# Stick-breaking attention in a hybrid block: three score banks, one out-projection bank, pairs finished by ScalarE and GpSimd

## The chip, the cores and the metric

The kernel runs on one core of a Trainium2 chip. The metric is the time of one execution on the device in microseconds, as the median of several runs. The core's engines are PE (TensorE, whose weight loads are shown as PEld), DVE (VectorE), ACT (ScalarE), POOL (GpSimd) and SP (SyncE, which here issues all DMAs of the kernel in one queue).

## What is computed

One decoder layer over 2048 tokens of width 1024, all in float32: an RMS norm, one input projection whose columns feed three mixers (a convolution branch, a gated unit with position mixing, and an attention of 8 heads of 64), an RMS norm of each branch, one output projection with a residual, then a gated feed-forward part and a final norm. The change acts in the attention and in the output projection behind it. Attention is of the stick-breaking kind:

```
z = q @ k.T * scale                      # scores of a 128-query block against all earlier keys
log_1m_beta = where(mask, -softplus(z), 0)
log_a = -softplus(-z) + reverse_cumsum(log_1m_beta) - log_1m_beta
a = where(mask, exp(log_a), 0)           # mask: strictly causal
o = a @ v
y = concat([rms(y_a), rms(y_b), rms(o)]) * g_out
x = x + y @ w_out
```

## The kernel before

Every matmul operand is split into a high and a low part, and each product is three matmuls (`mm3`, lines 114 to 117) or, with k and v, two. The work goes through stages, with tile pools opened and closed between them.

The first stage treats the sequence in two halves of 1024 tokens. For each it projects the columns of the two other mixers, then k, q and v, and stores q, k and v (as differences of neighbouring rows) to DRAM tensors `qh_d`, `ql_d`, `kh_d`, `kl_d` and `v_d`. When the second half is done, the operands of the first attention pair are loaded into four tiles `pre` of the pool that held x (lines 513 to 550), the outstanding pieces of the other branches are emitted, and the pools change.

The attention stage (lines 553 to 904) has 80 units: four blocks `qs` of 512 queries, four pairs `pr` of heads, chunks `kc` of 512 keys from the last to the first, and the two heads of the pair. Each unit has four steps, so there are 320 in one written order (loop at line 855). A step does three things. `front` (L709) makes a 128x512 block of scores in a PSUM bank of pool `zp` by two matmuls (L726, L729); ScalarE takes 1 - sigmoid of it into `om` (L731), and VectorE scans it along the keys (L739, or L734 with the mask on the diagonal chunk). The scan reads the bank, so it frees it. Six steps later `transpose_a` (L746) transposes a 128-key column of the four blocks of a unit and splits it into `ah` and `al`, the low part by VectorE from PSUM for even columns (L764) and by GpSimd from a copy for odd ones (L761). Eight steps later (`LAG_V`) `times_v` (L767) adds the products with v to one of two banks `po`, one for each head of the pair.

When a pair is through all its key chunks, `finish_pair` (L776) adds the two halves of each head's bank (ScalarE copies one, L783, VectorE adds the other, L784), adds `vend` (GpSimd, L787), scales by g_out and splits into `ych` and `ycl` (ScalarE L794, VectorE L795), stores both, and adds the squares to `sq` (ScalarE L802, VectorE L803). After four pairs `rms_c` turns `sq` into the branch's norm.

Between the steps the output projection runs as a filler: `out_proj` (L640) is a generator that emits three matmuls at a time into a bank `pab` of pool `opp`; after four such pieces VectorE adds the bank into the tile `x1` (L667 for the first two branches, L669 for attention). A debt of 0.6 pieces a step (1.8 in steps 14 to 31) decides when a piece is emitted, and a piece is issued behind the latest scores. What is left after the last step is emitted in one go (line 898), and the last block of attention's output projection follows (lines 901 and 975). A second generator, `down_blocks` (L592), runs every 20 steps from step 40 on: it loads two row blocks of w_down into tiles `wd0` and `wd1`, forms four combinations on GpSimd and stores them.

The program is written in this order, but each engine's queue is ordered by a list scheduler that simulates the time line, so that an instruction that is ready can be put ahead of ones written before it. Semaphores are placed by the framework. PSUM has eight banks: in this stage two each for scores (`zp`), output projection (`opp`), transposes (`atp`) and products with v (`otp`).

Of the kernel before, what the change touches and what calls it, by code (L numbers as in the profile page):

```python
# [15 lines left out]
P = 128  # L16
# [4 lines left out]
def kernel(  # L21
# [412 lines left out]

    for hf in range(2):
# [31 lines left out]
        for c0, hd, ld in ((1536, kh_d, kl_d), (1024, qh_d, ql_d)):  # L467
            w = load_w(c0)
            for ct in range(NPAIR):
# [43 lines left out]
    def load_q(tiles, qs, pr):  # L513
        qA, qB = tiles
        t_s = slice(qs * 512, (qs + 1) * 512)
        dma32(qA[0:64], qh_d[pr, 0:64, t_s])
        dma32(qA[64:128], ql_d[pr, 0:64, t_s])
        dma32(qB[0:64], ql_d[pr, 64:128, t_s])
        dma32(qB[64:128], qh_d[pr, 64:128, t_s])
        return tiles  # L520

    def load_kv(tiles, kc, pr):
        kA, kB, lA, lB, vv = tiles
        k_s = slice(kc * 512, (kc + 1) * 512)
        for hd, th_, tl_ in ((0, kA, lA), (1, kB, lB)):
            hr = slice(64 * hd, 64 * hd + 64)
            for r in (slice(0, 64), slice(64, 128)):
                dma32(th_[r], kh_d[pr, hr, k_s])
                dma32(tl_[r], kl_d[pr, hr, k_s])
        dma32(  # L530
            vv,
            v_d[kc * 4 : kc * 4 + 4, :, pr * 256 : (pr + 1) * 256].rearrange(
                "n p c -> p n c"
            ),
        )
        return tiles


    pre = [
        xp.tile([P, D], F32R, tag="xi", name=f"pre{i}").rearrange("p (a c) -> p a c", a=2)  # L540
        for i in range(4)
    ]
    first_q = load_q((pre[0][:, 0, :], pre[0][:, 1, :]), 0, 0)
    first_kv = load_kv(
        (
            pre[1][:, 0, :], pre[1][:, 1, :], pre[2][:, 0, :], pre[2][:, 1, :],
            pre[3].rearrange("p a (n c) -> p (a n) c", c=256),
        ),
        0, 0,
    )  # L550
# [8 lines left out]
    tp2 = pool(cr, "tp2", 3, "right")  # L559
    co = ExitStack()  # L560
    opp = pool(co, "opp", 2, "right", space=PSUM)
    zp = pool(cr, "zp", 2, "right", space=PSUM)
# [20 lines left out]
    def load_wo(f):  # L583
        raw = xo.tile([P, D], F32, tag="xo", name="rawo", bufs=3)
        nc.sync.dma_start(raw, w_out_r[f])
        wh = wo.tile([P, D], F32R, tag=f"woh{f}", name=f"woh{f}")
        wl = wo.tile([P, D], F32R, tag=f"wol{f}", name=f"wol{f}")
        split_pool(wh, wl, raw)
        wo_h.append(wh)
        wo_l.append(wl)  # L590

    def down_blocks():  # L592

        for f in range(NFH):
            r0 = xo.tile([P, D], F32, tag="wd0", name="wd0", bufs=1)
            r1 = xo.tile([P, D], F32, tag="wd1", name="wd1", bufs=1)
# [38 lines left out]
    def load_x1(n, g):  # L635
        x1 = xo.tile([P, D], F32, tag="xo", name="x1", bufs=3)
# [3 lines left out]
    def out_proj(qs, g, kept=()):  # L640
# [6 lines left out]
        for j in range(4):  # L647
            n = qs * 4 + j
            x1, (yh, yl) = nxt, ys.pop(0)
            for nh in range(2):  # L650
# [5 lines left out]
                ps = opp.tile([P, 512], F32, tag="opp", name="pab")  # L656
# [18 lines left out]
                if nh == 1 and g == 1:  # L675
# [99 lines left out]

    def finish_pair(p, sq):  # L776
        pr = p.pr
        yp = tp2.tile([P, 512], F32, tag="tmp", name="yp", bufs=2)
        tmp = tp2.tile([P, 512], F32, tag="tmp", name="tmp", bufs=2)
        for hd in range(2):  # L780
            hr = slice(64 * hd, 64 * hd + 64)
# [12 lines left out]
        A.mul(ych, yp, gc)  # L794
        V.scalar_tensor_tensor(ycl, yp, gc, ych, op0=ALU.mult, op1=ALU.subtract)  # L795
# [481 lines left out]
```

## Time and profile before

| | |
|---|---|
| median of 3 runs | 2570.83 us (2569.0 to 2572.99) |
| profiled execution, its own time | 2562.59 us |
| its span | 2560.5 us |
| TensorE clock granted, mean | 0.978 |
| PE busy | 2412.8 us (94%) |
| PEld busy | 1962.2 us (77%) |
| DVE busy | 1853.6 us (72%) |
| ACT busy | 1203.6 us (47%) |
| POOL busy | 1226.9 us (48%) |
| DMA moved | 445.68 MB |

The profile is one execution, its times are counted from the start of the span. Busy time of PE is modelled, since matmuls overlap in the array: a matmul of 512 columns is shown with about 0.39 us, but the next begins after 0.23 us. The share of a whole span says little here, as the stages have different limits; the attention stage lies between about 518 and 1190 us.

### The profile page before, as it was taken

To read this page: it belongs to the slowest core of one execution; us is meant where nothing else is said; L and a number is where in the kernel's file an instruction comes from. 1 tells how busy PE (TensorE), PEld (TensorE's weight loads), DVE (VectorE), ACT (ScalarE), POOL (GpSimd) and SP (SyncE) were. 2 spreads that over 40 slices of the span, in tenths; PEclk is the share of its full clock that TensorE was granted. 3 is DMA by queue.
4 is the path that set the end of the run, shared out by engine and by line. 5 is a ranking of instruction groups with operands and counts; after the bars stand their busy time and mean duration, and the time that the engine had idled before them with its cause. 6 is when DMAs were issued, how large, how long until landed. Compare 5 with 4: busy or idle time off the path is not lost.

```text
span 2560.5 us, 33221 instructions
## 1 busy us (share of the span) xinstructions
PE 2412.8 (94%) x11139; PEld 1962.2 (77%) x11139; DVE 1853.6 (72%) x2344; ACT 1203.6 (47%) x2130; POOL 1226.9 (48%) x929
## 2 busy tenths in 40 slices
PE   7999999968889899998799999999989999999998
PEld 5878778756767777777588888888877888888887
DVE  3881595357789899994588988875557888888555
ACT  4333522365567677773444444454344344345542
POOL 2434552454447647653144444565433444447551
PEclk9999999978999999999899999999999999999999
DMA  4245625399999898866433333397643333337962
GB/s 138 83 147 173 190 83 156 131 257 267 272 269 269 268 264 243 243 203 205 145 95 107 108 95 105 116 334 231 173 162 106 100 107 103 99 107 224 304 191 91
DMA packets 418073, 445.68 MB, mean 174 GB/s; under 512 B 24018, under 2 KB 301790, under 8 KB 417903
## 3 DMA queue, kind: packets, MB, share of 16 engines
q1 hardware_dynamic: 417903, 443.55, 58.6%
q8 instruction: 89, 1.46, 0.2%
q14 instruction: 81, 0.66, 0.1%
HBM read 305.57 MB, written 137.89 MB: 173 GB/s over the span
## 4 chain that ended last, share of the span: by engine, by line
PE 76%; DMA 9%; DVE 6%; POOL 3%; ACT 3%; issue 3%; SPq 1%; POOLq 0%; ACTq 0%; DVEq 0%
PE prod L116 11%; PE prod L115 11%; PE prod L117 11%; PE pd L116 6%; PE pd L115 6%; PE pd L117 5%; PE pjt L115 3%; PE pjt L117 3%; PE pjt L116 3%; PE pat L752 3%; DVE om L739 2%; PE pz L726 2%; PE po L774 1%; PE pjd L115 1%; PE pjd L116 1%
## 5 line engine op out<-in xcount | busy, mean ns | idle before, releaser
L121 POOL TENSOR_TENSOR wl<-raw,wh 128x512 fp32r<-128x512 f32 (+1 forms) x260 | 381.8, 1470 | 566.6 <-ACT wh L120 542.0
L115 PE MATMUL prod<-thh,wh 128*128 128x512 f32 x1232 | 482.9, 392 | 6.4 <-DVE thl L1008 5.8
L116 PE MATMUL prod<-thl,wh 128*128 128x512 f32 x1232 | 485.8, 394 | 0.3 <-DVE thl L1008 0.3
L117 PE MATMUL prod<-thh,wl 128*128 128x512 f32 x1232 | 482.5, 392 | 0.0
L120 ACT CAST wh<-raw 128x512 fp32r<-128x512 f32 (+1 forms) x260 | 178.0, 686 | 318.2 <-PE prod L116 178.2
L121 POOL TENSOR_TENSOR dwl<-raw,dwh 128x512 fp32r<-128x512 f32 x154 | 221.6, 1469 | 135.6 <-ACT dwh L120 95.6
L115 PEld LDWEIGHTS prod<-thh,wh 128*128 128x128 f32 x1232 | 232.1, 188 | 61.3 <-DVE thl L1008 7.8
L761 POOL TENSOR_TENSOR al<-ar,ah 128x512 fp32r<-128x512 f32 (+2 forms) x160 | 188.2, 1178 | 177.1 <-ACT ah L760 126.7
L116 PEld LDWEIGHTS prod<-thl,wh 128*128 128x128 f32 x1232 | 232.2, 188 | 50.6 <-DVE thl L1008 1.1
L117 PEld LDWEIGHTS prod<-thh,wl 128*128 128x128 f32 x1232 | 232.2, 188 | 48.9
L739 DVE TENSOR_TENSOR_SCAN om<-om,pz 128x512 f32<-128x512 f32 x192 | 239.6, 1270 | 36.4 <-ACT om L731 35.2
L116 PE MATMUL pd<-dwl,sah 128*128 128x512 f32 x616 | 242.1, 393 | 0.0
L115 PE MATMUL pd<-dwh,sah 128*128 128x512 f32 x616 | 240.8, 391 | 1.1 <-DVE thl L1008 1.0
L117 PE MATMUL pd<-dwh,sal 128*128 128x512 f32 x616 | 240.6, 391 | 0.0
L1126 DVE TENSOR_TENSOR sal<-ar,sah 128x512 fp32r<-128x512 f32 x168 | 154.2, 930 | 119.1 <-ACT sah L1125 108.5
L1066 DVE SCALAR_TENSOR_TENSOR cv<-u,vec,cv 128x1024 f32<-128x1024 f32 x176 | 222.6, 1287 | 14.1 <-ACT cv L1064 12.3
L731 ACT ACTIVATE om<-pz 128x512 f32<-128x512 f32 (+2 forms) x320 | 168.2, 545 | 89.9 <-PE pz L729 88.0
L1013 DVE TENSOR_TENSOR u<-prod,u 128x512 f32<-128x512 f32 x220 | 147.2, 686 | 64.2 <-PE prod L117 61.0
L752 PE MATMUL pat<-ident,om 128*128 128x128 f32 x1088 | 180.1, 281 | 8.7 <-DVE al L764 3.9
L752 PEld LDWEIGHTS pat<-ident,om 128*128 128x128 f32 x1088 | 138.5, 144 | 43.9 <-DVE al L764 7.6
L121 POOL TENSOR_TENSOR wl<-s,wh 128x512 fp32r<-128x512 f32 x88 | 122.7, 1394 | 98.0 <-ACT wh L120 98.0
L734 DVE TENSOR_TENSOR_SCAN om<-om,mask 128x128 f32<-128x128 f32 (+3 forms) x128 | 142.2, 1140 | 34.9 <-ACT om L731 34.6
(278 smaller groups left out, 5167.5 us busy)
## 6 DMA issues: line engine op xcount, KB each, us to landing
raw<-in_w_up_dram SPq DMA_DIRECT2D x88, 512.0 KB
ar<-s_d SPq DMA_DIRECT2D x112, 256.0 KB
s_d<-act SPq DMA_DIRECT2D x110, 256.0 KB
raw<-in_w_in_dram SPq DMA_DIRECT2D x40, 512.0 KB
raw<-wd_d SPq DMA_DIRECT2D x40, 512.0 KB
vv<-v_d SPq DMA_DIRECT2D x39, 512.0 KB
x_d<-x SPq DMA_DIRECT2D x32, 512.0 KB
raw<-in_w_down_dram SPq DMA_DIRECT2D x30, 512.0 KB
```

The costliest lines, as they stand in the source:

```text
L115: T.matmul(ps, lh, rh, start=start, stop=False)
L116: T.matmul(ps, lh, rl, start=False, stop=False)
L117: T.matmul(ps, ll, rh, start=False, stop=stop)
L120: A.copy(hi, src)
L121: G.tensor_tensor(lo, src, hi, op=ALU.subtract)
L731: A.activation(om, pz[:, :w_], AF.Sigmoid, scale=-0.125)
L739: V.tensor_tensor_scan(om[:, ::-1], om[:, ::-1], pz[:, ::-1], initial=p.carry[hd, j], op0=ALU.mult, op1=ALU.bypass,)
L752: T.transpose(pt[:, j * P : (j + 1) * P], a4[j][:, b * P : (b + 1) * P], ident)
L761: G.tensor_tensor(al[:, c_], ar[:, c_], ah[:, c_], op=ALU.subtract)
L1013: V.tensor_tensor(dst, ps, other, op=ALU.add)
L1066: V.scalar_tensor_tensor(cv, u[:, j : j + HALF], cw(j), cv, op0=ALU.mult, op1=ALU.add)
L1126: V.tensor_tensor(lo, ar, hi, op=ALU.subtract)
```

## The change

Seven edits are made together.

- Pool `zp` gets three banks and `opp` one; `zp` now closes together with `opp`, after the last output projection, whose accumulations (the last query block of attention) use `zp`.
- Finishing is split. `finish_head` runs behind a head's last product with v: ScalarE copies both halves of the bank to SBUF (`tmp` and `yp`), so a bank is read by ScalarE alone. `finish_pair` then adds them on GpSimd, adds `vend`, sums the squares on GpSimd, scales on GpSimd, copies to `ych` on ScalarE and takes the low part on GpSimd. The last pair of all keeps VectorE for these (`is_last`).
- `LAG_V` is 9 in place of 8, and the parts `ah` and `al` have four buffers in place of three.
- The operands of the first pair are loaded before the q projections of the second half rather than after its v projections. The helpers `load_q` and `load_kv` move up with them, unchanged.
- The tiles `wd0` and `wd1` are taken from the tag `xo`, which x1, the raw rows of w_out and `er` share; it has four buffers in place of three, and the two single buffers are gone.
- GpSimd's multiplication of h by `gffn_b` is done in two halves of 512 columns.
- In `finish_pair` the squares come before the scaling.

```diff
--- before.py
+++ after.py
@@ -432,6 +432,31 @@
             )
         dma32(v_d[n], vt.rearrange("p a b d -> p (a b d)"))
 
+    def load_q(tiles, qs, pr):
+        qA, qB = tiles
+        t_s = slice(qs * 512, (qs + 1) * 512)
...
+    def load_kv(tiles, kc, pr):
+        kA, kB, lA, lB, vv = tiles
...
     for hf in range(2):
 
         for ch in range(2):
@@ -466,6 +491,23 @@
 
         for c0, hd, ld in ((1536, kh_d, kl_d), (1024, qh_d, ql_d)):
             w = load_w(c0)
+            if hf == 1 and c0 == 1024:
+
+                pre = [
+                    xp.tile([P, D], F32R, tag="xi", name=f"pre{i}").rearrange(
+                        "p (a c) -> p a c", a=2
+                    )
+                    for i in range(4)
+                ]
+                first_q = load_q((pre[0][:, 0, :], pre[0][:, 1, :]), 0, 0)
+                first_kv = load_kv(
+                    (
+                        pre[1][:, 0, :], pre[1][:, 1, :], pre[2][:, 0, :],
+                        pre[2][:, 1, :],
+                        pre[3].rearrange("p a (n c) -> p (a n) c", c=256),
+                    ),
+                    0, 0,
+                )
             for ct in range(NPAIR):
                 for ch in range(2):
                     ps = proj_t(w, ct, hT[ch])
@@ -510,44 +552,6 @@
             w = load_w(0)
             nxt.append(transpose_x(xs))
             hT = nxt
-    def load_q(tiles, qs, pr):
...
-    def load_kv(tiles, kc, pr):
...
-    pre = [
...
-    first_q = load_q((pre[0][:, 0, :], pre[0][:, 1, :]), 0, 0)
...
     while later:
         tick()
     cr.close()
@@ -556,10 +560,10 @@
     cr = ExitStack()
     kv = pool(cr, "kv", 2, "right")
     ap_ = pool(cr, "ap", 1, "right")
-    tp2 = pool(cr, "tp2", 3, "right")
+    tp2 = pool(cr, "tp2", 4, "right")
     co = ExitStack()
-    opp = pool(co, "opp", 2, "right", space=PSUM)
-    zp = pool(cr, "zp", 2, "right", space=PSUM)
+    opp = pool(co, "opp", 1, "right", space=PSUM)
+    zp = pool(co, "zp", 3, "right", space=PSUM)
     cl.close()
     cl = ExitStack()
     wo = pool(cl, "wo", 1)
@@ -581,7 +585,7 @@
     wo_h, wo_l = [], []
 
     def load_wo(f):
-        raw = xo.tile([P, D], F32, tag="xo", name="rawo", bufs=3)
+        raw = xo.tile([P, D], F32, tag="xo", name="rawo", bufs=4)
         nc.sync.dma_start(raw, w_out_r[f])
         wh = wo.tile([P, D], F32R, tag=f"woh{f}", name=f"woh{f}")
         wl = wo.tile([P, D], F32R, tag=f"wol{f}", name=f"wol{f}")
@@ -592,8 +596,8 @@
     def down_blocks():
 
         for f in range(NFH):
-            r0 = xo.tile([P, D], F32, tag="wd0", name="wd0", bufs=1)
-            r1 = xo.tile([P, D], F32, tag="wd1", name="wd1", bufs=1)
+            r0 = xo.tile([P, D], F32, tag="xo", name="wd0", bufs=4)
+            r1 = xo.tile([P, D], F32, tag="xo", name="wd1", bufs=4)
             nc.sync.dma_start(r0, w_down_r[f])
             nc.sync.dma_start(r1, w_down_r[NFH + f])
             b11, b12, b21, b22 = r0[:, 0:512], r0[:, 512:D], r1[:, 0:512], r1[:, 512:D]
@@ -633,7 +637,7 @@
         return t
 
     def load_x1(n, g):
-        x1 = xo.tile([P, D], F32, tag="xo", name="x1", bufs=3)
+        x1 = xo.tile([P, D], F32, tag="xo", name="x1", bufs=4)
         nc.sync.dma_start(x1, x1_d[n] if g else xt[n])
         return x1
 
@@ -653,7 +657,10 @@
                     ys.append(load_y(n + 2, g, kept))
                 if nh == 1 and j < 3:
                     nxt = load_x1(n + 1, g)
-                ps = opp.tile([P, 512], F32, tag="opp", name="pab")
+                if g == 1 and qs == NQ - 1:
+                    ps = zp.tile([P, 512], F32, tag="zp", name="pab")
+                else:
+                    ps = opp.tile([P, 512], F32, tag="opp", name="pab")
                 for f in range(4):
                     if f < 4 - len(kept):
                         lh, ll = yh[:, f, :], yl[:, f, :]
@@ -685,7 +692,8 @@
                         )
                     else:
                         G.tensor_scalar(h, x1, r, 1.0, op0=ALU.mult, op1=ALU.mult)
-                        G.tensor_tensor(h, h, gffn_b, op=ALU.mult)
+                        for c in (slice(0, 512), slice(512, D)):
+                            G.tensor_tensor(h[:, c], h[:, c], gffn_b[:, c], op=ALU.mult)
                     if j % 2 == 0:
                         even = h
                     else:
@@ -773,38 +781,58 @@
         T.matmul(po[:, c_], vb, ah[:, c_], start=first, stop=False)
         T.matmul(po[:, c_], vb, al[:, c_], start=False, stop=kc == 0 and b == 3)
 
+    def finish_head(p, hd):
+
+        if hd == 0:
+            p.y = [
+                tp2.tile([P, 512], F32, tag="tmp", name=n, bufs=2) for n in ("yp", "tmp")
+            ]
+        yp, tmp = p.y
+        hr = slice(64 * hd, 64 * hd + 64)
+        other = slice(64 * (1 - hd), 64 * (1 - hd) + 64)
+        A.copy(tmp[hr], p.po[hd][other])
+        if is_last(p):
+            V.tensor_tensor(yp[hr], p.po[hd][hr], tmp[hr], op=ALU.add)
+        else:
+            A.copy(yp[hr], p.po[hd][hr])
+
+    def is_last(p):
+        return p.qs == NQ - 1 and p.pr == NPAIR - 1
+
     def finish_pair(p, sq):
         pr = p.pr
-        yp = tp2.tile([P, 512], F32, tag="tmp", name="yp", bufs=2)
-        tmp = tp2.tile([P, 512], F32, tag="tmp", name="tmp", bufs=2)
-        for hd in range(2):
-            hr = slice(64 * hd, 64 * hd + 64)
-            other = slice(64 * (1 - hd), 64 * (1 - hd) + 64)
-            A.copy(tmp[hr], p.po[hd][other])
-            V.tensor_tensor(yp[hr], p.po[hd][hr], tmp[hr], op=ALU.add)
+        yp, tmp = p.y
+        eng = V if is_last(p) else G
         y4 = yp.rearrange("p (j t) -> p j t", j=4)
         ve = vend[:, pr, 4 * p.qs : 4 * p.qs + 4]
-        G.tensor_tensor(y4, y4, ve.unsqueeze(2).to_broadcast([P, 4, P]), op=ALU.add)
+        if not is_last(p):
+            G.tensor_tensor(yp, yp, tmp, op=ALU.add)
+        eng.tensor_tensor(y4, y4, ve.unsqueeze(2).to_broadcast([P, 4, P]), op=ALU.add)
         if p.qs == 0:
 
             G.memset(yp[:, 0:1], 0.0)
         ych = yc.tile([P, 512], F32R, tag="ych", name="ych")
         ycl = yc.tile([P, 512], F32R, tag="ycl", name="ycl")
         gc = gout_c[:, 4 + pr : 5 + pr]
-        A.mul(ych, yp, gc)
-        V.scalar_tensor_tensor(ycl, yp, gc, ych, op0=ALU.mult, op1=ALU.subtract)
-        t_s = slice(p.qs * 512, (p.qs + 1) * 512)
-        dma32(yh_d[4 + pr, :, t_s], ych)
-        dma32(yl_d[4 + pr, :, t_s], ycl)
         if pr == 0:
             A.square(sq, yp)
         else:
             A.square(tmp, yp)
-            V.tensor_tensor(sq, sq, tmp, op=ALU.add)
+            eng.tensor_tensor(sq, sq, tmp, op=ALU.add)
+        if is_last(p):
+            A.mul(ych, yp, gc)
+            V.scalar_tensor_tensor(ycl, yp, gc, ych, op0=ALU.mult, op1=ALU.subtract)
+        else:
+            G.tensor_scalar(yp, yp, gc, 1.0, op0=ALU.mult, op1=ALU.mult)
+            A.copy(ych, yp)
+            G.tensor_tensor(ycl, yp, ych, op=ALU.subtract)
+        t_s = slice(p.qs * 512, (p.qs + 1) * 512)
+        dma32(yh_d[4 + pr, :, t_s], ych)
+        dma32(yl_d[4 + pr, :, t_s], ycl)
         return ych, ycl
 
     def load_vend():
-        er = xo.tile([P, D], F32, tag="xo", name="er", bufs=3)[:NKB, 0 : NPAIR * P]
+        er = xo.tile([P, D], F32, tag="xo", name="er", bufs=4)[:NKB, 0 : NPAIR * P]
         nc.sync.dma_start(
             er, vr_d[1 : S + 1].rearrange("(n p) c -> n p c", p=P)[:, P - 1, :]
         )
@@ -841,7 +869,7 @@
     anchor = [None]
     sqs, rcs = {}, {}
     debt = 0.0
-    LAG_T, LAG_V = 6, 8
+    LAG_T, LAG_V = 6, 9
 
 
     WO_0, WO_S = 2, 3
@@ -889,6 +917,8 @@
             qs, pr, kc, hd = units[u]
             p = pairs[qs, pr]
             times_v(p, kc, hd, b, *parts_t.pop((u, b)))
+            if kc == 0 and b == 3:
+                finish_head(p, hd)
             if kc == 0 and hd == 1 and b == 3:
                 if pr == 0:
                     sqs[qs] = yb_.tile([P, 512], F32, tag="sq", name="sq", bufs=1)
```

## Rows read from the trace of the kernel before

**Rows 1.** Three stretches: us, each engine busy (instructions), granted clock, DMA share, GB/s.
```profile
525.00:775.00 250.00, 210.90 (x1028) 167.63 (x1029) 183.69 (x222) 148.26 (x323) 120.70 (x104) 0.90 1.01 267
775.00:1125.00 350.00, 325.92 (x1744) 261.55 (x1743) 315.88 (x344) 252.25 (x511) 231.68 (x180) 0.99 0.89 253
...
1160.00:1180.00 20.00, 20.00 (x101) 16.63 (x100) 7.05 (x10) 5.58 (x10) 4.24 (x4) 1.00 0.42 146
```
**Rows 2.** The sigmoid alone (L731) in two of them: ACT busy (instructions), then as above.
```profile
525.00:775.00 250.00, 53.81 (x110) 0.90 1.01 267
775.00:1125.00 350.00, 101.72 (x187) 0.99 0.89 253
```
**Rows 3.** Chain of waits, shares by line, from 525 to 775 and from 775 to 1125.
```profile
by line: DMA yh<-yh_d 7.3%; DMA wd<-in_w_down_dram 7.2%; DMA yl_d<-ycl 5.9%; DVE om L734 5.7%; DMA kB<-kh_d 5.4%; SPq L91 4.9%; PE pat L752 4.7%; DMA x<-in_x_dram 3.9%; issue 3.7%; DMA kA<-kh_d 3.4%; DMA yl<-yl_d 3.3%; DMA rawo<-in_w_out_dr
by line: PE pat L752 12.2%; DVE om L739 9.8%; PE pz L726 7.7%; PE po L774 7.0%; PE pz L729 6.5%; PE po L773 6.5%; issue 5.3%; DVE om L734 5.2%; PE pab L115 4.4%; PE pab L117 4.4%; PE pab L116 4.4%; DVE al L764 2.4%; POOL al L761 2.0%; DMA h
```
**Rows 4.** PE's waits from 775 to 1150: us in total, times, longest.
```profile
PE pz L726 <- DVE om L739: 11.8, 21, 3.5
PE po L774 <- POOL al L761: 7.1, 6, 2.6
PE pat L752 <- DVE al L764: 3.4, 4, 1.2
```
**Rows 5.** Groups of VectorE: operation, count, busy us, mean ns, idle before.
```profile
L784 DVE TENSOR_TENSOR yp<-po,tmp 64x512 f32<-64x512 f32 x32 | 21.8, 680 | 5.2 <-ACT tmp L783 4.6
...
L795 DVE SCALAR_TENSOR_TENSOR ycl<-yp,vec,ych 128x512 fp32r<-128x512 f32 x16 | 13.8, 864 | 4.6 <-ACT ych L794 4.6
...
L803 DVE TENSOR_TENSOR sq<-sq,tmp 128x512 f32<-128x512 f32 x12 | 10.6, 886 | 0.0
```
**Rows 6.** Groups of GpSimd, the same columns.
```profile
L423 POOL TENSOR_TENSOR vp<-vp,vs 128x512 f32<-128x512 f32 x16 | 21.2, 1326 | 39.5 <-DMA vp<-vr_d 29.5 <-ACT om L731 7.6 <-ACT xc L367 1.2
L787 POOL TENSOR_TENSOR yp<-yp,vend 128x512 f32<-128x512 f32 x16 | 17.0, 1062 | 30.4 <-DVE yp L784 17.3 <-ACT ah L760 7.1 <-PE pz L729 6.1
...
L687 POOL TENSOR_SCALAR h<-x,r_ffn 128x1024 f32<-128x1024 f32 x12 | 14.1, 1179 | 0.9
```
**Rows 7.** PE's waits from 525 to 775, first and last of eight for engines.
```profile
PE po L774 <- DVE al L764: 6.0, 7, 2.6
...
PE pat L752 <- DVE om L734: 1.4, 3, 0.6
```
**Rows 8.** A wait of ScalarE from 525 to 1190.
```profile
ACT ych L794 <- POOL yp L787: 10.3, 11, 1.9
```
**Rows 9.** Time line of the flush: start, us, instruction; first and last eviction.
```profile
1161.40 0.39 PE L115 MATMUL pab<-woh,yh 128*128 128x512 f32 x1
1161.60 0.69 DVE L667 TENSOR_TENSOR x<-pab,x 128x512 f32<-128x512 f32 x1 [0.67 <-PE pab L117]
...
1173.45 0.69 DVE L667 TENSOR_TENSOR x<-pab,x 128x512 f32<-128x512 f32 x1 [2.54 <-PE pab L117]
```
**Rows 10.** Time line of PE in the last out-projection; the idle time before stands in brackets.
```profile
1197.50 0.50 PE L115 MATMUL pab<-woh,yh 128*128 128x512 f32 x1 [1.52 <-DVE x L669]
```
**Rows 11.** First operands: a load's row (count, ns, first and last start) and the first score.
```profile
L91 SPq DMA_DIRECT2D pre<-qh_d x2: 545/585/625, 296.4 to 299.1; - x2
...
518.52 0.29 PEld L726 LDWEIGHTS pz<-pre,pre 128*128 128x128 f32 x1 [7.63 <-ACT vs L497]
```
**Rows 12.** Issues of w_down's and x1's tiles (as Rows 11), and VectorE's wait for x1.
```profile
L597 SPq DMA_DIRECT2D wd<-in_w_down_dram x11: 333/577/1192, 602.8 to 999.8; - x11
...
L674 SPq DMA_DIRECT2D x_d<-x x32: 319/452/924, 591.2 to 1217.7; - x32
...
DVE x L667 <- DMA x<-in_x_dram: 7.3, 2, 5.0
```
**Rows 13.** Scans with the mask: ns least, median, most of all; and the narrowest group.
```profile
L734 DVE TENSOR_TENSOR_SCAN om<-om,mask x128: 402/1193/2242, 519.6 to 1111.8; 128x128 f32<-128x128 f32 x32, 128x256 f32<-128x256 f32 x32, 128x384 f32<-128x384 f32 x32, 128x512 f32<-128x512 f32 x32
...
L734 DVE TENSOR_TENSOR_SCAN om<-om,mask 128x128 f32<-128x128 f32 x32 | 25.6, 798 | 14.8 <-ACT om L731 14.7
```

More of the change, by code (lines that the diff above doesn't have):

```diff
@@ L433, in v_steps @@
         dma32(v_d[n], vt.rearrange("p a b d -> p (a b d)"))
+    def load_q(tiles, qs, pr):
+        qA, qB = tiles
+        t_s = slice(qs * 512, (qs + 1) * 512)
+        dma32(qA[0:64], qh_d[pr, 0:64, t_s])
+        dma32(qA[64:128], ql_d[pr, 0:64, t_s])
+        dma32(qB[0:64], ql_d[pr, 64:128, t_s])
+        dma32(qB[64:128], qh_d[pr, 64:128, t_s])
+        return tiles
+    def load_kv(tiles, kc, pr):
+        kA, kB, lA, lB, vv = tiles
+        k_s = slice(kc * 512, (kc + 1) * 512)
+        for hd, th_, tl_ in ((0, kA, lA), (1, kB, lB)):
+            hr = slice(64 * hd, 64 * hd + 64)
+            for r in (slice(0, 64), slice(64, 128)):
+                dma32(th_[r], kh_d[pr, hr, k_s])
+                dma32(tl_[r], kl_d[pr, hr, k_s])
+        dma32(
+            vv,
+            v_d[kc * 4 : kc * 4 + 4, :, pr * 256 : (pr + 1) * 256].rearrange(
+                "n p c -> p n c"
+            ),
+        )
+        return tiles
     for hf in range(2):
@@ L468 @@
             w = load_w(c0)
+            if hf == 1 and c0 == 1024:
[11 more added lines that the diff above has]
+                        pre[3].rearrange("p a (n c) -> p (a n) c", c=256),
+                    ),
+                    0, 0,
+                )
             for ct in range(NPAIR):
@@ L512 @@
             hT = nxt
-    def load_q(tiles, qs, pr):
[L514 to L520, printed above, removed]
-    def load_kv(tiles, kc, pr):
-        kA, kB, lA, lB, vv = tiles
-        k_s = slice(kc * 512, (kc + 1) * 512)
-        for hd, th_, tl_ in ((0, kA, lA), (1, kB, lB)):
-            hr = slice(64 * hd, 64 * hd + 64)
[L527 to L536, printed above, removed]
-    pre = [
-        xp.tile([P, D], F32R, tag="xi", name=f"pre{i}").rearrange("p (a c) -> p a c", a=2)
-        for i in range(4)
-    ]
-    first_q = load_q((pre[0][:, 0, :], pre[0][:, 1, :]), 0, 0)
[L544 to L550, printed above, removed]
     while later:
@@ L774, in times_v @@
         T.matmul(po[:, c_], vb, al[:, c_], start=False, stop=kc == 0 and b == 3)
+    def finish_head(p, hd):
[4 more added lines that the diff above has]
+        yp, tmp = p.y
+        hr = slice(64 * hd, 64 * hd + 64)
+        other = slice(64 * (1 - hd), 64 * (1 - hd) + 64)
[6 more added lines that the diff above has]
+        return p.qs == NQ - 1 and p.pr == NPAIR - 1
     def finish_pair(p, sq):
         pr = p.pr
[L778 to L784 removed]
+        yp, tmp = p.y
+        eng = V if is_last(p) else G
         y4 = yp.rearrange("p (j t) -> p j t", j=4)
         ve = vend[:, pr, 4 * p.qs : 4 * p.qs + 4]
[L787 removed]
+        if not is_last(p):
+            G.tensor_tensor(yp, yp, tmp, op=ALU.add)
+        eng.tensor_tensor(y4, y4, ve.unsqueeze(2).to_broadcast([P, 4, P]), op=ALU.add)
         if p.qs == 0:
```

## The prediction

> **What bounds the kernel now.** I read the slices first: the attention stage runs from about 518 to 1190 us, and it is the only place where every edit acts. Then I cut that stage into stretches [rows 1]. From 525 to 775 the DMA engines show a share of 1.01 at 267 GB/s while PE is busy for 210.9 of 250 us; from 775 to 1125 DMA falls to 0.89, and PE (325.9 of 350 us) and VectorE (315.9) are both near full; from 1160 to 1180 PE is busy without a gap and VectorE nearly idle. So there are three different limits. The sigmoid at L731 runs once per step (one 128-query block of scores), so its count gives the pace [rows 2]: 110 in 250 us, 2.27 us a step, then 187 in 350 us, 1.87 us a step. The chain of waits says the same [rows 3]: in the first stretch its largest items are transfers, in the second they are transposes, scans and matmuls in turn, none over 12.2%. In the second stretch PE and VectorE are therefore coupled, and the waits of PE show through what [rows 4]: 11.8 us in 21 times for a scan (L739) to free a score bank, 7.1 us for GpSimd's low parts (L761), 3.4 us for VectorE's (L764).
>
> **The change part by part.** The sum is made against the profiled execution (2562.59 us, span 2560.5, 2.1 us around it); the median of the three runs is 2570.83, 8.2 above it, and I subtract the saving from that.
>
> *Finishing moved off VectorE, and the third score bank.* Per pair VectorE loses two additions of 0.680, one low part of 0.864 and, in three pairs of four, one sum of squares of 0.886 [rows 5]: 1.36 + 0.86 + 0.66 = 2.89 us. Fifteen of 16 pairs change, 43 us in all; the last keeps VectorE. Some seven of them end between 775 and 1150 (L784 stands there 14 times, two a pair), so 20 us there. VectorE's 315.9 us over 187 steps are 1.69 us a step and become about 1.58; PE's 325.9 are 1.74 and stay. VectorE then has slack, PE is the slower one, and a third bank lets it run one block further ahead of the scans. The 11.8 us can go at most; since the longest single wait was 3.5 us, more than a step, I leave 3 and take -9 (bounds 0 and -12). What is late next is PE itself, whose idle time in that stretch is 350 - 326 = 24 us: no more than that can come back there.
>
> *Products with v a step later, four buffers for the parts.* The low parts get 1.87 us more. The row of 7.1 us has six waits, 1.2 on average and 2.6 at most, so the extra step would cover nearly all; with the 3.4 of VectorE's low parts 10.5 us are in reach. But GpSimd gets a burst per pair: a new addition near 1.33 (L423 has its form), the addition of vend as now (1.06), a sum of squares and a low part near 1.33 each, and a multiplication near 0.59 (half of L687's 1.18) [rows 6], 5.6 us in place of 1.06. Fifteen times 4.6 is 69 us on an engine busy for 352 of 600 us [rows 1]. I take a good half, -6 (bounds 0 and -11).
>
> *The same two in the first stretch.* PE waits there for engines in eight rows, 6.0 us down to 1.4, 22.8 in all [rows 7]. With DMA at 1.01 most of what one wait gives back the next transfer takes, as nothing in the change moves fewer bytes. I take -4 (bounds 0 and -20).
>
> *ScalarE.* Per pair two copies of 64x512 more, 0.58 each; the scaled copy becomes a plain one. They lie in ScalarE's idle time (252 of 350 us busy). But ScalarE now waits for GpSimd twice in a pair (square after vend, copy after the multiplication) where it waited once, 10.3 us in 11 times [rows 8], and the sigmoids stand behind it. Score banks that are a block ahead hide most; +2 (bounds 0 and +10, one more such row). That GpSimd's multiplication by gffn_b is cut in halves only lets a low part in between: 0.
>
> *One out-projection bank.* A bank now has to be evicted before the next group of 12 matmuls can begin. I compared the rows of all 53 evictions with the start of the next group: between 775 and 1160 both overlap in four places, 1.1 us together, since the next group comes a step or two later. It bites where the backlog is flushed: PE begins the next group at 1161.40, the eviction of the one before runs from 1161.60 for 0.69 [rows 9], and four of the five evictions there are like that, near 0.9 us each. 4 x 0.9 + 1.1 = +5 with the way of a semaphore (bounds 0, if other matmuls fill the gaps, and +8, if groups come faster). It is on the path, since PE is full there.
>
> *The last out-projection on three banks, the last pair.* The wait of 1.52 us at 1197.5 for an eviction [rows 10] goes and vend is added by VectorE; -2 (bounds 0 and -3).
>
> *First operands ahead of v.* They are not late now: the loads are issued from 296 us on, though they stand behind v in the text, and the first score starts at 518.5 after a wait of 7.63 for the last copy of v (L497), which frees a score bank's space [rows 11]. The edit moves 13 issues past SP's queue at a place where it has room, and that copy stays: 0 (bounds -8, should another bank come first, and +2).
>
> *The tiles of w_down in the pool of x1.* Four buffers for both, before three and two. One block's pair of tiles is held long: 11 loads from 602.8 to 999.8, 40 us apart [rows 12], so two buffers are almost always w_down's and x1 is left with two. A tile of x1 is stored every 20 us (32 from 591.2 to 1217.7) and the next is loaded half a tile ahead, so two should just do: 0; the other end is the second rival below.
>
> Sum: -9 - 6 - 4 + 2 + 5 - 2 = -14 us, 2548.6 for the profiled execution, **2557** for the median.
>
> VectorE's scans that read om and mask from SBUF take 0.402 at the shortest, and those of 128x128 0.798 on average [rows 13]; something holds them for as long again. By the Trainium skill (SBUF — State Buffer, Who interferes with whom) a VectorE instruction with two SBUF inputs contends with a GpSimd instruction that reads SBUF, and the second to start blocks until the first is done. The trace agrees with it, and the rule speaks against the change: with 0.4 us lost in each of 128 scans at the present 352 us of GpSimd work (an estimate from that row), 69 us more would cost VectorE 128 x 0.4 x 69/352 = 10 us, which leaves 33 of its 43; by the rule alone the sum would be some 3 us smaller.
>
> **The rivals.** *The transfers decide.* If SP's queue and the DMA engines set the pace after 775 too (0.89 is not far from 1), VectorE's relief turns into idle time and only the flush and the tail remain, +5 - 2: 2574, within 0.2%. For it speaks the first stretch; against it, that transfers are hardly in the second chain [rows 3]. Chance 0.19.
>
> *GpSimd becomes the wait (slower).* Place: L761's low part queued behind a pair's burst. Price: 4.6 us more burst less the 1.87 of the added step, 2.7 us a pair, and 15 times 2.7 is 41 us on PE, against which the 20 us of the two first terms stay at best half: 41 - 10 = +31 with the +3 of the bank and the tail, near 2602 if every burst stands whole; half of them gives 2585. It decides where GpSimd runs three or more of the five without a low part in between. For it: 232 of 350 us busy already. Against it: the burst waits for ScalarE twice, which lets low parts in. Chance 0.12, at 2585.
>
> *x1 late for its eviction (slower).* With two buffers an x1 load waits for a store of the block before it, the one bank stays full, and PE stands. VectorE waited 7.3 us in two times for x already, 5.0 the longer [rows 12]. Eight tiles late by 3.6 us, less the 14: +15, 2586. Chance 0.09.
>
> *More comes back.* If PE's 24 us of idle time after 775 all go and the first stretch gives 10: -24 - 10 + 5 = -29, 2542. Chance 0.15. My forecast has 0.45.
>
> **How the numbers follow.** Another 0.2%, 5 us, is about what a measurement of this kernel can tell. The forecast's own range is 2548 to 2566; with bounds and rivals 2530 to 2588. Faster: 0.45 and 0.15, 0.60; same: 0.19; slower: 0.21.
>
> **What would show it.** Right: PE's wait for L739 in the second stretch near 3 us and the step under 1.82; VectorE's busy time in the stage about 40 us lower and GpSimd's about 70 higher; gaps near 0.9 between groups in the flush. Wrong: a row of PE waiting for L761 over 15 us, VectorE waiting for x1, a DMA share of 1 throughout, or a first score well before or after 518.5. A step of 1.87 or more after 775 would refute the first two terms.

## The result: slower, and the profile after

The changed kernel takes 2582.92 us (2579.45 to 2586.41, five runs) against 2569.0 us (2561.53 to 2572.99, five runs) of the kernel before beside it: ratio 1.0064, 95% interval 1.0042 to 1.0086. The forecast was 14 us faster; by the medians it came out 14 us slower. The time lies in the outer range (2530 to 2588) and not in the forecast's own (2548 to 2566), and it moved the other way. The profiled execution took 2586.41 us, its span is 2584.7, 24.2 longer than the one of before, at a mean granted clock of 0.975. The two profiled executions thus stand further apart than the medians; what follows accounts for the 24.2 us between them.

The same stretches in the profile after, in the columns of [rows 1]; the last one now lies 20 us later, where the flush went.

```profile
525.00:775.00 250.00, 205.99 (x1015) 163.74 (x1013) 175.25 (x193) 150.85 (x336) 158.19 (x131) 0.90 0.97 266
775.00:1125.00 350.00, 312.77 (x1619) 243.11 (x1617) 272.10 (x291) 228.51 (x479) 238.70 (x200) 0.98 0.81 240
1180.00:1210.00 30.00, 30.00 (x154) 24.92 (x153) 11.79 (x15) 9.39 (x18) 6.47 (x5) 1.00 0.35 114
```

The sigmoid alone (now L739), in the columns of [rows 2]:

```profile
525.00:775.00 250.00, 53.93 (x114) 0.90 0.97 266
775.00:1125.00 350.00, 89.67 (x171) 0.98 0.81 240
```

The first stretch has four steps more than before (114 for 110), the second 16 fewer: 171 in 350 us are 2.05 us a step, where it was 1.87. In that stretch PE is busy for 13.2 us less, VectorE for 43.8 (some 20 of them the finishing that it gave away), ScalarE for 23.7, and the DMA share fell from 0.89 to 0.81. Only GpSimd, which took the finishing over, has more, by 7.0 us, and it is busy for 238.70 of 350. So no engine and no transfer is fuller than PE was before; something that couples them got slower. By 1050 us 249 sigmoids are done, where it was 261 before: 12 steps of 2.05 us make 25 us, about the whole difference of the spans.

The waits in the second stretch, after (us in total, times, longest). L739 is the sigmoid, L747 the scan, L760 the transposes, L768 and L771 the casts `ah`, L769 and L772 the low parts `al` by GpSimd and VectorE, L782 the products with v, L676 the eviction of the output projection.

```profile
DVE al L772 <- ACT ah L771: 58.4, 34, 5.1
...
ACT om L739 <- PE pat L760: 20.4, 19, 3.2
...
PE pz L734 <- DVE om L747: 16.9, 33, 2.6
...
PE po L782 <- POOL al L769: 9.0, 9, 2.5
PE pat L760 <- DVE al L772: 7.3, 10, 2.6
```

And of before, in the same stretch, where L731 is the sigmoid, L729 the scores, L763 and L764 the cast and VectorE's low part:

```profile
ACT om L731 <- PE pz L729: 33.4, 60, 2.2
...
PE pz L726 <- DVE om L739: 8.0, 19, 1.2
...
DVE al L764 <- ACT ah L763: 1.2, 4, 0.7
```

Two waits are new. VectorE stands 58.4 us for the cast whose low part it is to take, where it stood 1.2. And the sigmoid waits 20.4 us for a *transpose*, which it never did before: a transpose is what frees a tile `om` for the sigmoid, so at these places the 13 tiles of `om` (the ring that the sigmoids fill in turn) are all in use. The wait that the third bank was to remove, PE's for the scan, doubled (16.9 for 8.0).

One place in the time line of after, ScalarE, VectorE and one instruction of PE from 1114 on (start, us, instruction, idle time before in brackets):

```profile
1114.54 0.59 ACT L771 CAST ah<-pat 128x512 fp32r<-128x512 f32 x1 [0.92 <-PE pat L760]
1115.15 0.69 DVE L772 TENSOR_TENSOR al<-pat,ah 128x512 fp32r<-128x512 f32 x1 [1.69 <-ACT ah L771]
1115.57 1.57 ACT L739 ACTIVATE om<-pz 128x512 f32<-128x512 f32 x3 [0.45 <-PE pat L760]
1116.20 2.45 DVE L747 TENSOR_TENSOR_SCAN om<-om,pz 128x512 f32<-128x512 f32 x2 [0.36 <-ACT om L739]
...
1117.54 0.50 PE L734 MATMUL pz<-kB,qB 128*128 128x512 f32 x1 [0.28 <-DVE om L747]
```

It reads as one loop: transposes, cast, low part, then sigmoids that need the tiles those transposes freed, then scans, then scores that need the scans' banks. Each link waits for the one before it. In the stretch of before no sigmoid waits for a transpose, so this loop was not closed there.

How far the front of a step is ahead of its back, its lead, can be counted in the trace: sigmoids up to a time, less casts up to it. Here L739, L768 and L771 of after, from 515 to 950 and to 1050 us:

```profile
515.00:950.00 435.00, 98.75 (x201) 0.92 0.92 259
515.00:1050.00 535.00, 124.90 (x249) 0.93 0.90 256
...
515.00:950.00 435.00, 46.99 (x94) 0.92 0.92 259
515.00:1050.00 535.00, 60.48 (x119) 0.93 0.90 256
...
515.00:950.00 435.00, 51.08 (x95) 0.92 0.92 259
515.00:1050.00 535.00, 65.10 (x120) 0.93 0.90 256
```

and L731, L760 and L763 of before:

```profile
515.00:950.00 435.00, 105.72 (x208) 0.93 0.97 267
515.00:1050.00 535.00, 134.72 (x261) 0.94 0.95 263
...
515.00:950.00 435.00, 49.41 (x101) 0.93 0.97 267
515.00:1050.00 535.00, 64.61 (x128) 0.94 0.95 263
...
515.00:950.00 435.00, 53.71 (x101) 0.93 0.97 267
515.00:1050.00 535.00, 69.11 (x128) 0.94 0.95 263
```

After: 201 - 189 = 12 and 249 - 239 = 10 steps; before: 6 and 5. As a mean over 650, 750, 850, 950 and 1050 us the lead is 11.6 after and 5.2 before, and the products with v (L782, L774 before) run 14.2 and 7.4 steps behind the sigmoids. The written distance is 6 for the transposes in both. The list scheduler decides the order in the queues. A reading that fits, though no trace shows the scheduler at work: with a third bank it finds a score ready earlier and puts it ahead, again and again, until the next resource is full, which is the ring of `om`. The theory to test: the third bank costs time through this lead. Rivals: GpSimd's longer finishing, late tiles of x1, the single out-projection bank.

### The profile page after: what moved, and what is told of

It is laid out like the page before. It is cut to its first block, busy times and chain, and to the rows that moved or that the text cites. A ratio compares the mean times of both kernels' runs of the same rounds, so it can differ in the third digit from the quotient of the medians.

```text
span 2584.7 us, 33408 instructions
## 1 busy us (share of the span) xinstructions
PE 2424.7 (94%) x11139; PEld 1961.7 (76%) x11139; DVE 1822.7 (71%) x2289; ACT 1203.3 (47%) x2160; POOL 1295.1 (50%) x996
## 4 chain that ended last, share of the span: by engine, by line
PE 76%; DMA 10%; DVE 6%; POOL 3%; issue 2%; ACT 2%; SPq 1%; POOLq 0%; ACTq 0%; DVEq 0%
PE prod L115 11%; PE prod L116 11%; PE prod L117 11%; PE pd L115 5%; PE pd L116 5%; PE pd L117 5%; PE pjt L115 3%; PE pjt L116 3%; PE pjt L117 3%; PE pat L760 2%; DVE om L747 2%; PE pz L734 2%; PE pab L115 2%; PE pab L116 1%; PE pab L117 1%
## 5 line engine op out<-in xcount | busy, mean ns | idle before, releaser
L769 POOL TENSOR_TENSOR al<-ar,ah 128x512 fp32r<-128x512 f32 (+2 forms) x160 | 185.1, 1158 | 160.8 <-ACT ah L768 135.9
L747 DVE TENSOR_TENSOR_SCAN om<-om,pz 128x512 f32<-128x512 f32 x192 | 235.2, 1264 | 11.2 <-ACT om L739 10.8
L1096 DVE SCALAR_TENSOR_TENSOR cv<-u,vec,cv 128x1024 f32<-128x1024 f32 x176 | 222.5, 1286 | 14.2 <-ACT cv L1094 12.5
L760 PE MATMUL pat<-ident,om 128*128 128x128 f32 x1088 | 176.5, 282 | 17.7 <-DVE al L772 15.1
L739 ACT ACTIVATE om<-pz 128x512 f32<-128x512 f32 (+2 forms) x320 | 162.6, 548 | 56.5 <-PE pat L760 34.5
L760 PEld LDWEIGHTS pat<-ident,om 128*128 128x128 f32 x1088 | 136.6, 144 | 58.4 <-DVE al L772 23.6
L772 DVE TENSOR_TENSOR al<-pat,ah 128x512 fp32r<-128x512 f32 (+1 forms) x160 | 99.7, 624 | 103.1 <-ACT ah L771 103.0
```

Source lines behind the costliest of these rows:

```text
L739: A.activation(om, pz[:, :w_], AF.Sigmoid, scale=-0.125)
L747: V.tensor_tensor_scan(om[:, ::-1], om[:, ::-1], pz[:, ::-1], initial=p.carry[hd, j], op0=ALU.mult, op1=ALU.bypass,)
L760: T.transpose(pt[:, j * P : (j + 1) * P], a4[j][:, b * P : (b + 1) * P], ident)
L769: G.tensor_tensor(al[:, c_], ar[:, c_], ah[:, c_], op=ALU.subtract)
L1096: V.scalar_tensor_tensor(cv, u[:, j : j + HALF], cw(j), cv, op0=ALU.mult, op1=ALU.add)
```

## The experiments

The ratios and their 95% intervals compare each kernel with runs of the kernel before beside it; they differ a little from the quotients of the medians. The lead is the mean at the five times above.

```
                                          us       ratio  interval          lead
after                                     2582.92  1.0064 1.0042 to 1.0086  11.6
before + banks (3 and 1)                  2599.76  1.0142 1.0129 to 1.0155  11.6
after with the old banks (2 and 2)        2541.93  0.9921 0.9904 to 0.9939   5.4
after, lead held near 6                   2541.91  0.9910 0.9894 to 0.9927   6.6
after, 10 tiles of om                     2568.43  1.0014 1.0002 to 1.0026   9.4
after, lead held near 9                   2551.45  0.9952 0.9933 to 0.9970   9.6
before + finishing                        2547.89  0.9935 0.9910 to 0.9960   5.0
before + LAG_V 9, buffers, shared pool    2553.59  0.9951 0.9933 to 0.9968   5.0
before + shared pool                      2561.97  0.9993 0.9974 to 1.0011   5.2
before + banks, lead held near 6          2548.31  0.9936 0.9914 to 0.9959   6.8
after, lead held near 6, 10 tiles of om   2527.75  0.9853 0.9828 to 0.9879   6.8
after, LAG 5 and 8, lead held near 5      2545.81  0.9924 0.9902 to 0.9946   5.8
before, lead held near 6                  2552.03  0.9952 0.9933 to 0.9970   5.4
```

**The banks alone, added to before.**

```diff
-    opp = pool(co, "opp", 2, "right", space=PSUM)
-    zp = pool(cr, "zp", 2, "right", space=PSUM)
+    opp = pool(co, "opp", 1, "right", space=PSUM)
+    zp = pool(co, "zp", 3, "right", space=PSUM)
...
+                if g == 1 and qs == NQ - 1:
+                    ps = zp.tile([P, 512], F32, tag="zp", name="pab")
```

> The kernel before with one part of the change: three score banks, one out-projection bank. Theory (lead): with a third bank the planned order puts the scores about 11 steps ahead of the parts of the same unit, where before it was 5, and the ring of 13 om tiles is full; the sigmoid then waits for transposes. This part alone gives the whole loss and, without VectorE's relief, more: ratio 1.008 to 1.016 (20 to 40 us), ScalarE's sigmoid waiting over 20 us for transposes, the step after 775 us near 2.0 us or more. Rival (GpSimd): the loss comes from the pairs' finishing on GpSimd, which is not in this kernel: ratio 0.996 to 1.002. Rival (one out-projection bank): the single bank is paid here too, PE waits for evictions of x: 5 to 15 us, ratio 1.002 to 1.006, and the step stays near 1.87.

2599.76 us, ratio 1.0142: the banks cost 35 us by themselves, more than the whole change. The step takes 2.07 us (169 in 350), and over the whole stage the sigmoid waits 25.9 us for transposes, as expected. PE's waits for evictions, the price of the single out-projection bank, come to 1.2 us. Its waits in the second stretch (L764 and L767 are the low parts, L766 the cast, L734 the sigmoid, L755 the transposes, L742 the scan):

```profile
DVE al L767 <- ACT ah L766: 27.9, 19, 3.6
...
ACT om L734 <- PE pat L755: 12.9, 16, 1.8
...
PE pz L729 <- DVE om L742: 16.1, 36, 2.3
...
PE po L777 <- POOL al L764: 3.3, 5, 1.8
```

Both new waits are there without any of the other edits, and PE hardly waits for GpSimd. So the loss comes neither from the finishing nor from the shared pool of x1.

**After with the old banks**: the reverse of this diff.

> The changed kernel with two score banks and two out-projection banks as before; finishing, lag, shared tiles and early loads stay changed. Theory (lead): the planned lead is back at 5 steps, the sigmoid no longer waits for transposes, and VectorE's relief shows: ratio to the kernel before 0.992 to 0.999. Rival (GpSimd): bursts of the finishing still hold the low parts: ratio 1.004 or more, PE waiting over 20 us for GpSimd's low parts. Rival (x1 late in the shared tiles): ratio over 1.003 with VectorE waiting for x over 15 us.

2541.93 us, 0.9921: everything but the banks makes the kernel 0.8% faster, and the banks on top of it cost 1.0064 / 0.9921, 1.4%, as alone. The waits in its second stretch (L736 sigmoid, L768 and L769 cast and low part, L779 products):

```profile
ACT om L736 <- PE pz L734: 27.6, 56, 1.9
...
PE po L779 <- POOL al L766: 13.4, 10, 4.0
...
DVE al L769 <- ACT ah L768: 7.3, 5, 4.5
...
PE pz L731 <- DVE om L744: 5.0, 13, 0.9
```

No sigmoid waits for a transpose.

**The lead held.** The scores of a step are put in PE's queue behind the transposes written one step earlier; all banks and buffers are those of after.

```diff
-            T.transpose(
+            tail[0] = T.transpose(
...
-            a4s.setdefault(u, []).append(front(pairs[qs, pr], kc, hd, j))
+            if s_ - 1 in tails:
+                with tc.issue_after(tails[s_ - 1].ins):
+                    a4s.setdefault(u, []).append(front(pairs[qs, pr], kc, hd, j))
...
+            tails[s_] = tail[0]
```

> The changed kernel with all its parts, three score banks among them, but the scores of a step are issued on PE behind the transposes written one step before, so that the lead stays at 6 steps. Theory (lead): it is the order, not the number of banks, that costs: ratio to the kernel before 0.990 to 1.000, sigmoid waits for transposes under 5 us. Rival (one out-projection bank): the bank is still single: ratio stays near 1.006. Rival (GpSimd): ratio near 1.006 as well.

2541.91 us, 0.991: some 40 us come back with the three score banks and the single out-projection bank in place. Its second stretch (columns of [rows 1]) and its waits there:

```profile
775.00:1125.00 350.00, 332.16 (x1813) 271.21 (x1814) 312.48 (x331) 263.13 (x547) 260.13 (x218) 0.99 0.87 258
```
```profile
PE po L782 <- POOL al L769: 16.2, 16, 3.5
...
DVE al L772 <- ACT ah L771: 8.4, 10, 3.3
...
PE pat L760 <- DVE al L772: 1.0, 3, 0.5
```

VectorE's wait for the cast fell from 58.4 to 8.4, and the rows of a sigmoid waiting for a transpose and of a score waiting for a scan are gone: this is what the third bank was to do, and PE is now busy for 332.2 of 350 us. Not all of it is the bank's loss undone, since the hold has a worth of its own (below).

**A smaller ring, and a lead between.** Two edits on after: `bufs=13` of `om` to 10; and the hold with `s_ - 4` in place of `s_ - 1`.

> The changed kernel with 10 om tiles in place of 13, so that the scores can be planned 8 steps ahead at most (11 in the changed kernel). Theory (lead, by the full ring): the ring is full at any length, so the sigmoid's waits for transposes stay or grow (30 us or more) and the time is equal or worse: ratio to the kernel before 1.004 to 1.015. A second form of the theory (the lead itself costs, by what stands in the queues between a score and its use, not the full ring): the shorter lead gives back a good part, ratio 1.000 to 1.004. Rivals (GpSimd, one out-projection bank): no change from the changed kernel, 1.005 to 1.008.

> The changed kernel with its ring of 13 om tiles, and the lead of the scores over the transposes held at 9 steps (6 in the kernel that held it shortest, 11 in the changed kernel; with a ring of 10 tiles it was planned at 8). Theory A (the lead costs by the full ring: with all om tiles in use every late transpose stops the sigmoid, and with it the casts and the low parts behind it): here 9 of 13 leave four tiles free, so the sigmoid waits little for transposes, and the time is that of the lead of 6: ratio to the kernel before 0.988 to 0.995. Theory B (the lead costs by itself, by what stands in the queues between a score and its use): 9 steps cost as with the ring of 10, ratio 0.999 to 1.004.

They have nearly the same lead, 9.4 and 9.6; in the first the ring is full (sigmoids wait for transposes 13.5 us in the second stretch), in the second there is no such row. They give 1.0014 and 0.9952, with intervals apart. This does not show that a full ring costs, because the two differ in the hold as well, and the hold brings 0.5% on the kernel before without a change of the lead (below). Nor do the expectations decide it: the first result lies in the range of the form in which the lead itself costs, the second just above that of the full ring. Of the two held kernels with 13 tiles the one with the shorter lead is faster: 0.991 at 6.6 against 0.9952 at 9.6, again with intervals apart. VectorE's wait for the cast is 58.4, 37.1, 16.1 and 8.4 us in the second stretch at leads of 11.6, 9.4, 9.6 and 6.6, but it does not follow the lead everywhere: in the last two kernels of this section it is 20.6 at 5.8 and 16.0 at 6.8.

**The other edits one at a time, on before.** Finishing by ScalarE and GpSimd (`finish_head`, `finish_pair`, `is_last` of the change):

```diff
+            if kc == 0 and b == 3:
+                finish_head(p, hd)
```

> The kernel before with the finishing of pairs moved to ScalarE and GpSimd, nothing else. As predicted with the change (VectorE 43 us lighter, the score banks still two): gain of some 10 us, ratio 0.993 to 0.999. Rival (GpSimd's burst): the low parts come late with the lag of 8, ratio 1.000 to 1.006, PE's wait for GpSimd's low parts from 775 to 1125 us rising from 7 to over 12 us.

2547.89 us, 0.9935: 16 us. The row that it was aimed at, PE's wait for the scan, falls only from 8.0 to 5.4 us in the second stretch; where the rest comes from stays open. The later products, with the buffers and the pool that they come with:

```diff
-    tp2 = pool(cr, "tp2", 3, "right")
+    tp2 = pool(cr, "tp2", 4, "right")
...
-    LAG_T, LAG_V = 6, 8
+    LAG_T, LAG_V = 6, 9
```

> The kernel before with products a step later, four buffers for the parts and, for their room, w_down's tiles in the shared pool. If the later products are worth what was predicted (6 us and some of the first stretch): ratio 0.994 to 0.999. If the shared pool holds x1 back: above 1.002 with VectorE waiting for x. If the planned order, in which the products already stood 6 steps behind, makes the lag moot: 0.999 to 1.001.

The pool of x1 and w_down alone (`bufs=3` to `bufs=4`, `wd0` and `wd1` on the tag `xo`):

> The kernel before with w_down's tiles in the shared pool of four, nothing else. Predicted as nothing: ratio 0.998 to 1.002. Rival (x1 late): 1.003 to 1.008.

0.9951 and 0.9993: the pool is worth nothing that can be measured, the later products with their buffers 0.4%, with intervals that don't overlap. The gains do not add up: 0.9935 and 0.9951 multiply to 0.9886, while all edits but the banks gave 0.9921. The early loads and GpSimd's halved multiplication were not run alone.

**Is it the bank or the hold?** The hold was put on before with the three banks, and on before as it was.

> The kernel before with three score banks and one out-projection bank alone, as in the first experiment (ratio 1.0142), but with the scores issued behind the transposes of the step before, which holds the lead at 6. Theory (lead): all of the 36 us goes and what is left is the worth of the banks themselves, a few us either way: ratio 0.994 to 1.003. Rival (the single out-projection bank has a price of its own): ratio 1.004 or more.

> The kernel before with nothing but the hold: the scores of a step stand in PE's queue behind the transposes written one step earlier; two score banks, two out-projection banks, finishing as before. It tells apart what brought the 0.9936 of the three banks with the lead held. If the third bank itself brings it, once the lead is held, the hold alone does nothing, as the lead before is 5.2 steps and the hold allows 6: ratio 0.998 to 1.002. If the hold brings it (an order of the queues that is better than the one planned freely), the ratio is 0.992 to 0.996 and the third bank is worth nothing or little in any order. If two banks need the freedom, the hold costs: over 1.003.

0.9936 and 0.9952, the first just better than its expected range. The hold brings 0.5% even with two banks, where it changes the mean lead by nothing (5.4 against 5.2): the freely planned order is not the best one either. Its 187 sigmoids in the second stretch are those of before; the first has 116 in place of 110. With the order held, the third score bank with the single out-projection bank makes a difference of 0.16%, within the intervals. In the free order it cost 1.42%. So the loss is shown to come through the order of the queues, and not from the banks themselves. What in that order costs, the long lead, the full ring or something else that the hold changes, these runs do not separate.

**The other way round: shorter lags, and a smaller ring with the hold.** After with `LAG_T, LAG_V = 5, 8` and the hold; after with the hold and 10 tiles of `om`.

> The changed kernel with the lead held at 5 steps: transposes written 5 steps and products 8 steps behind the scores, the scores issued behind the transposes of the step before. If a shorter lead goes on paying: ratio 0.985 to 0.990. If 6 was short enough and the low parts now come just in time: 0.990 to 0.996.

> The changed kernel with the lead held at 6 steps and a ring of 10 om tiles, so that four tiles are free as in the kernel with the lead of 9 and 13 tiles (ratio 0.9952); with the lead of 6 and 13 tiles it was 0.991. If free tiles in the ring decide: 0.994 to 0.997. If the lead itself costs beyond the full ring: 0.989 to 0.993.

0.9924 and 0.9853. The shorter lag gives nothing more than 6.6 did. The smaller ring with the hold is the fastest of all, 2527.75 us, better than both kernels. It beats the same kernel with 13 tiles by 0.6%, although the lead is the same (6.8, 6.6) and in neither trace a sigmoid waits for a transpose; it lies below both expected ranges, and the theory that free tiles as such help is refuted by it. Why it is faster stays open: the two profiled executions have spans of 2529.1 and 2530.6 us, so they do not show the difference of their medians.

## Why the prediction was wrong, point by point

- **The step that failed** is the third score bank in "Finishing moved off VectorE, and the third score bank". It was to let PE "run one block further ahead of the scans" and was bounded "0 and -12": a free bank was taken as something that can only remove a wait. With the single out-projection bank it costs +35 us alone. The queues are ordered by a scheduler, and the prediction priced every edit as if their order stayed; the lead went from 5.2 to 11.6 steps, and PE's wait for the scan in the second stretch, to go to 3 us, went from 8.0 to 16.9.
- That the measured time lies near two of the slower rivals (2585 and 2586) is luck: neither of their mechanisms made the loss, as the next points show.
- The finishing in the same term was right in direction and too small: alone it brings 16 us, where the whole term had 9. VectorE's busy time fell by 30.9 us (1853.6 to 1822.7), GpSimd's rose by 68.2, the second near the 70 forecast, the first short of the 40 (the last section says where some of it went). GpSimd's added groups (operation, count, busy us, mean ns, idle before):

```profile
L828 POOL TENSOR_TENSOR ycl<-yp,ych 128x512 fp32r<-128x512 f32 x15 | 21.3, 1420 | 4.3 <-ACT ych L827 4.3
L809 POOL TENSOR_TENSOR yp<-yp,tmp 128x512 f32<-128x512 f32 x15 | 20.3, 1353 | 7.8 <-ACT yp L797 6.0 <-PE pz L737 1.6 <-PE pat L760 0.2
...
L821 POOL TENSOR_TENSOR sq<-sq,tmp 128x512 f32<-128x512 f32 x11 | 15.4, 1401 | 3.2 <-ACT tmp L820 3.2
L826 POOL TENSOR_SCALAR yp<-yp,vec 128x512 f32<-128x512 f32 x15 | 13.7, 912 | 1.3 <-ACT sq L818 1.3
```

  They make 70.7 us; the multiplication takes 0.91, not the 0.59 taken as half of L687's.
- *Products a step later*: worth about 10 us with their buffers, like the -6 and -4, but not in the way they said, so the agreement is luck. In the kernel with this edit on before the products run 7.2 steps behind the sigmoids, 7.4 without it: a lag written one longer didn't move them, and PE's wait for L761 in the second stretch is 18.6 us there, 7.1 in [rows 4]. Where its gain comes from stays open.
- *ScalarE* (+2): its waits for GpSimd in the finishing are shorter than the 10.3 us of [rows 8]: 5.8 us in the whole stage, the longest rows 2.3 and 2.0. No loss is seen.
- *One out-projection bank* (+5) and *the last out-projection* (-2): PE waits for an eviction four times between 400 and 1250 us, 7.2 us in all, against 1.5 once before. That is near the price that was named, but it is not paid in the flush: PE is busy for 30.00 of 30 us there. The wait of [rows 10] didn't go: the last of the four is

```profile
1228.92 0.63 PE L115 MATMUL pab<-woh,yh 128*128 128x512 f32 x1 [1.35 <-DVE x L676]
```

- *First operands* (0): no gain is seen, as forecast, though no run has the edit alone. The first score begins at 520.90 after a wait of 7.44 us for the same kind of copy of v (now L539), 518.52 and 7.63 in [rows 11].
- *The pool of x1* (0): right, by the run with it alone.
- *GpSimd becomes the wait*: its row is there, 22.0 us from 560 to 1185 where 15 were named as the mark, and 9.3 before. But the kernel with the old banks has 24.1 and the one with the lead held 32.3, and both are faster than before. A row of waiting over a mark did not tell what bounds. (The rival's 2602 leaves out the +3 that it names: 41 - 10 + 3 is 34, near 2605.)
- *Transfers decide* and *x1 late*: the DMA share fell to 0.81, and VectorE waited for loads before x1's sum twice, 8.0 and 1.0 us, where it was 7.3 in two times [rows 12]. Neither.
- The mark that did work: "A step of 1.87 or more after 775 would refute the first two terms". It is 2.05. It does not say which part of them failed: alone, the finishing and the later products both gain, and the banks lose.

## What to carry to other kernels

Where a scheduler orders the queues, a buffer that is added at one place can change the order everywhere; ask first how far the stage in front of it will run ahead, and which ring stops it. Count the lead in the trace (front instructions less back instructions up to a time), and tie the front to the back explicitly before a buffer is judged: here the same third bank costs 1.4% in the free order and next to nothing in the held one. Run the tie alone as well, because it can be worth something itself (0.5% here). And price an edit that "can only help" from both sides.

## What the runs showed of the hardware

The scans that read `om` and `mask` from SBUF are held up by GpSimd, which has more to do after the change. Those of after, by width (columns of [rows 5]):

```profile
L742 DVE TENSOR_TENSOR_SCAN om<-om,mask 128x512 f32<-128x512 f32 x32 | 54.9, 1714 | 2.5 <-ACT om L739 2.5
L742 DVE TENSOR_TENSOR_SCAN om<-om,mask 128x384 f32<-128x384 f32 x32 | 43.9, 1373 | 4.7 <-ACT om L739 4.6
L742 DVE TENSOR_TENSOR_SCAN om<-om,mask 128x256 f32<-128x256 f32 x32 | 29.6, 924 | 5.7 <-ACT om L739 5.6
L742 DVE TENSOR_TENSOR_SCAN om<-om,mask 128x128 f32<-128x128 f32 x32 | 28.1, 878 | 6.6 <-ACT om L739 6.5
```

They sum to 156.5 us, those of before to 145.9. In the profiles of all kernels here the sums are 139.9 to 148.3 (mean of six 144.3) where VectorE finishes the pairs, and 144.4 to 158.6 (mean of eight 152.8) where GpSimd does. The means lie 8.5 us apart, but the groups overlap: 144.4 is the kernel with the lead held near 9, 148.3 the one with the shared pool alone. So 43 us were taken from VectorE and about 10 seem to be given back in its scans, which agrees with its busy time (-30.9) and with the 10 us that the prediction estimated for it.

What holds a scan up can be read in the trace of after, from two scans of 512 columns, each with the GpSimd instruction that it overlaps, and a free GpSimd instruction of the second one's kind:

```profile
1014.26 1.94 POOL L608 TENSOR_TENSOR wd<-wd 128x512 f32<-128x512 f32 x1
1015.03 2.25 DVE L742 TENSOR_TENSOR_SCAN om<-om,mask 128x512 f32<-128x512 f32 x1
...
1078.45 1.20 DVE L742 TENSOR_TENSOR_SCAN om<-om,mask 128x512 f32<-128x512 f32 x1
1078.88 1.85 POOL L769 TENSOR_TENSOR al<-ar,ah 128x512 fp32r<-128x512 f32 x1 [3.56 <-ACT ah L768]
...
1017.92 1.28 POOL L769 TENSOR_TENSOR al<-ar,ah 128x512 fp32r<-128x512 f32 x1
```

The first scan starts while GpSimd is at work and takes 2.25 us; it ends 1.08 us after GpSimd does. The second starts first and takes 1.20, and GpSimd's instruction takes 1.85 where 1.28 will do. So it is throughout: of the 128 scans of after, 51 start while no GpSimd instruction runs, and none of these takes over 0.43, 0.70, 0.96 or 1.23 us at widths of 128, 256, 384 and 512; the other 77 take up to 2.45, 1.94, 2.41 and 2.25. In the trace of before it is 58 and 70, with the same four limits. The 192 scans whose second input is a PSUM bank (least, median and most in ns) are not held up in either kernel:

```profile
L747 DVE TENSOR_TENSOR_SCAN om<-om,pz x192: 1246/1266/1282, 607.8 to 1188.3; 128x512 f32<-128x512 f32 x192
```

By the Trainium skill (SBUF — State Buffer, Who interferes with whom), a VectorE instruction with two SBUF inputs contends with a GpSimd instruction that reads SBUF. The trace agrees, and in these rows whichever starts second takes longer. How much of the 10.6 us between before and after comes from GpSimd's added work, and how much from the other order of the queues, no run separates.
